# Where the tiles of a two-layer decoder trunk lie in SBUF

## The chip, the cores and the metric

The kernel runs on one core of one Trainium2 chip. What counts is its device time in microseconds. Several runs are timed, and the median is compared.

## What is computed

Two layers of a decoder trunk on one sequence of 512 tokens with 1,024 features, in float32. `c` is one vector of 1,024 that conditions the layer.

```python
for layer in range(DEPTH):
    mod = silu(c) @ w_ada[layer] + b_ada[layer]            # nine vectors of 1024
    sh1, sc1, g1, sh2, sc2, g2, sh3, sc3, g3 = split(mod)
    h = modulate(rmsnorm(x, norm_g[layer, 0]), sh1, sc1)
    x = x + 0.5 * g1 * ((silu(h @ w1) * (h @ w3)) @ w2)     # d_ff = 2816
    h = modulate(rmsnorm(x, norm_g[layer, 1]), sh2, sc2)
    proj = h @ w_in[layer]                                  # 3656 columns
    ...                                                     # 4 + 4 + 8 heads: block attention, top-k attention, stick-breaking
    x = x + g2 * (headnorm(concat(oa, ob, oc)) @ w_out[layer])
    h = modulate(rmsnorm(x, norm_g[layer, 2]), sh3, sc3)
    x = x + 0.5 * g3 * ((silu(h @ w1b) * (h @ w3b)) @ w2b)
```

## The kernel before

Everything is kept with features on the 128 partitions and the 512 tokens along them: the residual `xs` is 8 tiles of 128 x 512. To keep the precision of float32, each operand of a large product is split into two parts, a rounded one and the rest, both in the format fp32r: `whi` and `wlo` for weights, `hh` and `hl` for the normed input h, `gh` and `gl` for a chunk of d_ff. `mm3` (L309 to L311) then makes three matmuls of each block, whi with hh, whi with hl, wlo with hh. The weight part is loaded into PE, the other one moves through it, 512 columns at a time.

Weights come in pieces of 128 x 1,024. `fetch` (L269, L271) starts a DMA on SyncE's queue into one of three `raw` tiles, and ScalarE casts it to `whi`. `load_piece` (L281) lets VectorE subtract to get `wlo`. There are five buffers of each.

The order of time is: FFN 1 of layer 0, the mixing stage, FFN 2, the same for layer 1. A FFN has two halves of 11 chunks of d_ff. In a half each chunk is made by `mm3` from h (the first products, w1 and w3, 8 steps each), then by SiLU and a multiplication (L495, L497), and split into `gh` and `gl` (L500, L501). After 11 chunks the second product (w2) runs: for each of 8 output tiles of 128 features, `mm3` over the 11 chunks with `gh` and `gl` moving, and an update of `xs` (L513). The last two output tiles of the second half go in two column halves of 256. In between VectorE makes the modulation vectors from `adaw` tiles (L356). In the mixing stage an order written out by hand (PLAN) interleaves projections, score matmuls (L620, tiles `qk`), products with v (L664, tiles `att` moving and `v` loaded) and cumulative sums (L713, constants `rmat`).

SBUF is given out by pools. A pool is a stretch of the same byte range in all partitions. The pools that live all the time are stacked from low addresses up in the order in which they are opened; the pool of a stage (`fp` for the FFNs, `mp` for mixing) is opened above them, closed, and the next stage's pool takes the same bytes. A tile of the new pool waits until the old tiles under it are released. Within a pool each name gets its number of buffers times its size, in the order of first use. This gives, in bytes of a partition:

| tiles | before |
|---|---|
| xs, modulation vectors, constants (rmat, causal, ones) | 1,152 to 24,128 |
| raw, 3 x 4,096 | 24,128 to 36,416 |
| whi, 5 x 4,096 | 36,416 to 56,896 |
| wlo, 5 x 4,096 | 56,896 to 77,376 |
| hh, 8 x 2,048 | 77,376 to 93,760 |
| hl, 8 x 2,048 | 93,760 to 110,144 |
| small ones (nacc, rsqrt, sums) | 110,144 to 113,600 |
| FFN stage, from 113,600 | |
| gh, 14 x 2,048 | from 125,888 (first FFN), 138,176 (second and third), 134,080 (last) |
| gl, 14 x 2,048 | from 154,560, 166,848, 162,752 |
| adaw, 3 x 4,096 | 183,232 to 207,808; in the first stage six, from 117,696 |
| mixing stage, from 113,600 | |
| tok, v | 118,208 to 126,400; 126,528 to 142,912 |
| tf, qk, att | 142,912 to 157,248; 161,344 to 185,920; 185,920 to 214,592 |

The 14 slots of gh and gl (11 in use, 3 more) are handed out in turn: first slot 0, then from 13 downwards.

Of the kernel before, what the change touches and what calls it, by code (L numbers as in the profile page):

```python
# [19 lines left out]
F32R = mybir.dt.float32r  # L20
# [6 lines left out]
P = 128  # L27
S = 512
# [5 lines left out]
HALF = NF // 2  # L34
# [42 lines left out]
def col(i):  # L77
    return ((i * P, (i + 1) * P),)


def head_chunks(l, f):

    return list(range(4 if (l, f) == (0, 0) else 2))
# [99 lines left out]
class Net:  # L183
    def __init__(self, tc, ctx, io):
        self.tc, self.nc, self.ctx, self.io = tc, tc.nc, ctx, io
        self.n = 0
        self.cp = ctx.enter_context(tc.tile_pool(name="consts", bufs=1))
        self.wp = ctx.enter_context(tc.tile_pool(name="weights", bufs=1))
        self.hp = ctx.enter_context(tc.tile_pool(name="acts", bufs=1))
        self.sp = ctx.enter_context(tc.tile_pool(name="tiny", bufs=1))  # L190
        pp = ctx.enter_context(tc.tile_pool(name="psum", bufs=1, space=PSUM))
        self.bank = lambda tag, shape: self.t(pp, tag, shape, bufs=2)
        self.new_z = lambda: self.t(pp, "z", [P, 1024], bufs=3)
        self.xs = self.cp.tile([P, KC, S], F32, name="xs")
        self.x = [self.xs[:, k, :] for k in range(KC)]
        self.piece, self.fetched = -1, None
        self.queue, self.delayed = [], []
        self.logs = False
        self.order = ExitStack()
# [45 lines left out]
    def setup_late(self):  # L245
        nc, cp = self.nc, self.cp
        self.outg, self.qkg, self.gcol, self.rope = self.load("late", False)
        for p in (0, HD):
            nc.gpsimd.memset(self.gcol[p:p + RD], 1.0)
        for i in (0, 2):  # L250
            nc.gpsimd.tensor_scalar(self.gcol[:, :, i], self.gcol[:, :, i], HD ** -0.5, None, op0=ALU.mult)
        self.rmat = cp.tile([P, 4, P], F32R, name="rmat")
        m = self.t(self.wp, "raw", [P, 4, P], bufs=3)
        nc.sync.dma_start(m, self.io["cmat"][:, 0:4, :])
        nc.vector.tensor_copy(self.rmat, m)
        self.identr, self.tri, self.nones, self.maskc = (self.rmat[:, i, :] for i in range(4))
        self.ident = self.identr.bitcast(F32)
        self.causal = cp.tile([P, S], F32, name="causal")
        nc.gpsimd.memset(self.causal[:, :S - P], 0.0)
        nc.sync.dma_start(self.causal[:, S - P:], self.io["cmat"][:, 4, :])  # L260


    def fetch(self):

        nc = self.nc
        self.piece += 1
        n = sum(sum(b - a for a, b in blk[3]) for blk in PIECES[self.piece])
        raw = self.t(self.wp, "raw", [P, 1024], bufs=3)
        nc.sync.dma_start(raw[:, :n], self.io["w"][self.piece, :, :n])  # L269
        hi = self.t(self.wp, "whi", [P, 1024], F32R, bufs=5)  # L270
        nc.scalar.copy(hi[:, :n], raw[:, :n])  # L271
        self.fetched = n, raw, hi
# [206 lines left out]
    def ffn(self, l, f, filler, head):  # L479

        nc = self.nc
        full = slice(0, S)
        for hf in range(2):
            g = []
            for fc in range(hf * HALF, (hf + 1) * HALF):
                if fc in head_chunks(l, f):
                    pp = head[2 * fc:2 * fc + 2]
                else:
                    pp = self.z_banks(1)
                    for w, ps in zip(("ffn_w1", "ffn_w3"), pp):  # L490
                        for k in range(KC):
                            wt = self.weight(w, (l, f), k, col(fc))
                            self.mm3(ps, wt, self.h[k], k == 0, k == KC - 1)
                sl = self.t(self.fp, "sil", [P, S], bufs=2)
                nc.scalar.activation(sl, pp[0], AF.Silu)  # L495
                gf = self.t(self.fp, "gf", [P, S], bufs=2)
                nc.vector.tensor_mul(gf, sl, pp[1])  # L497
                hi = self.t(self.fp, "gh", [P, S], F32R, bufs=HALF + 3)
                lo = self.t(self.fp, "gl", [P, S], F32R, bufs=HALF + 3)
                nc.scalar.copy(hi, gf)  # L500
                nc.vector.tensor_sub(lo, gf, hi.bitcast(F32))  # L501
                g.append((hi, lo))
                if fc not in head_chunks(l, f):
                    next(filler, None)
            gate = self.mod[l, 2 if f == 0 else 8]

            def products(ps, ws, cs):
                for j in range(HALF):
                    self.mm3(ps[:, cs], ws[j], [p[:, cs] for p in g[j]],
                             j == 0 and cs.start == 0, j == HALF - 1, skip_group_check=cs != full)  # L510

            def update(m, ps, cs):
                nc.vector.scalar_tensor_tensor(self.x[m][:, cs], ps[:, cs], gate[:, m:m + 1],  # L513
                                               self.x[m][:, cs], op0=ALU.mult, op1=ALU.add)

            if hf == 1:
                self.norm_begin()
            w2 = lambda m: [self.weight("ffn_w2", (l, f), hf * HALF + j, col(m)) for j in range(HALF)]
            whole = KC - (TAIL if hf == 1 else 0)
            for m in range(whole):  # L520
                if m % 2 == 0:
                    pss = self.z_banks(1)
                ps = pss[m % 2]
                for j in range(HALF):
                    wt = self.weight("ffn_w2", (l, f), hf * HALF + j, col(m))
                    self.mm3(ps, wt, g[j], j == 0, j == HALF - 1)
                update(m, ps, full)
                if hf == 1:
                    yield m, full
            if whole == KC:  # L530
                continue
            last = list(zip(range(whole, KC), map(w2, range(whole, KC)), self.z_banks(TAIL)[::2]))
            for cs in HALVES:
                for m, ws, ps in last:
                    products(ps, ws, cs)
                    update(m, ps, cs)
                    yield m, cs

    def open_ffn(self, es):
        self.fp = es.enter_context(self.tc.tile_pool(name=self.name("fp"), bufs=1))  # L540
        self.temp = lambda: self.t(self.fp, "nt", [P, S], bufs=6)

# [616 lines left out]
```

## Time and profile before

| | |
|---|---|
| time, median of 3 runs | 2143.43 us (2143.17 to 2144.86) |
| the profiled execution, its own time | 2149.0 us |
| its span, first to last instruction | 2147.1 us |
| mean granted TensorE clock | 0.996 |
| PE busy | 2096.4 us, 98% |
| weight loads (PEld) | 1806.7 us, 84% |
| DVE busy | 1289.2 us, 60% |
| ACT busy | 837.4 us, 39% |
| DMA | 281.74 MB, mean 131 GB/s |

Times within a profile are microseconds from the start of the span. PE is the matmul side of TensorE, PEld its weight loads, which overlap PE. Matmuls are pipelined: the record of one is longer than the distance to the next, so the pace is read from start to start. A source line such as L309 is a line of a helper, which many callers share; the names of the tiles (out<-in) tell them apart.

### The profile page before, as it was taken

The page shows a single profiled execution, that of the slowest core. Times are in us where ns is not written, and L with a number is a line of the kernel's source. Part 1 is how long each engine was busy: PE and PEld are TensorE (multiplying, and loading weights), DVE is VectorE, ACT ScalarE, POOL GpSimd, SP SyncE. Part 2 cuts the span into 40 slices and gives each one's busy share as a digit, 9 for nine tenths or more (in the row PEclk, how much of TensorE's full clock was granted, in tenths as well). Part 3 has the DMA queues.
Part 4 walks back from the last instruction along what each step waited for, and adds up shares of the span by engine and source line. Part 5 has one row for each costly group of instructions (what it writes and reads, how often), then busy time and mean ns, then how long its engine had stood idle before and what let it go on. Part 6 is the DMA issues. An engine that isn't in the chain of part 4 may idle for free.

```text
span 2147.1 us, 28606 instructions
## 1 busy us (share of the span) xinstructions
PE 2096.4 (98%) x11280; PEld 1806.7 (84%) x11280; DVE 1289.2 (60%) x2425; ACT 837.4 (39%) x1347; POOL 3.5 (0%) x12
## 2 busy tenths in 40 slices
PE   6999999999999999999999999999999999999999
PEld 5888888888998888888898888888889998888888
DVE  8772753679978777275374333346899776333332
ACT  3321222467675432122242222324776644222220
POOL 0000000000000000000000000000000000000000
PEclk9999999999999999999999999999999999999999
DMA  7783853342333378386334333324334223333331
GB/s 297 264 283 98 265 171 89 103 107 67 100 91 103 112 262 279 98 269 199 90 105 132 98 98 96 93 82 122 91 84 106 74 71 108 98 89 99 98 102 56
DMA packets 86149, 281.74 MB, mean 131 GB/s; under 512 B 10752, under 2 KB 13312, under 8 KB 86016
## 3 DMA queue, kind: packets, MB, share of 16 engines
q1 hardware_dynamic: 84576, 277.83, 42.3%
q8 instruction: 88, 1.44, 0.3%
q10 hardware_dynamic: 1440, 2.10, 0.3%
q14 instruction: 45, 0.37, 0.1%
HBM read 256.55 MB, written 2.10 MB: 120 GB/s over the span
## 4 chain that ended last, share of the span: by engine, by line
PE 84%; DVE 10%; ACT 3%; DMA 2%; issue 1%; SPq 0%; ACTq 0%; DVEq 0%
PE z L309 23%; PE z L311 23%; PE z L310 23%; PE b L309 3%; PE b L311 3%; PE b L310 3%; DVE sc L862 2%; DVE m L861 2%; PE z L620 1%; DVE att L575 1%; DMA qk<-qk 1%; DVE wlo L281 1%; PE z L664 1%; PE z L713 1%; DVE tf L725 1%
## 5 line engine op out<-in xcount | busy, mean ns | idle before, releaser
L281 DVE TENSOR_TENSOR wlo<-raw,whi 128x1024 fp32r<-128x1024 f32 (+1 forms) x338 | 412.4, 1221 | 534.0 <-ACT whi L271 532.0
L271 ACT CAST whi<-raw 128x1024 fp32r<-128x1024 f32 (+1 forms) x338 | 354.3, 1049 | 863.1 <-PE z L310 791.8
L309 PE MATMUL z<-hh,whi 128*128 128x512 f32 (+1 forms) x1616 | 597.6, 371 | 6.9 <-DVE xs L996 3.9
L310 PE MATMUL z<-hl,whi 128*128 128x512 f32 (+1 forms) x1616 | 597.5, 370 | 0.5
L311 PE MATMUL z<-hh,wlo 128*128 128x512 f32 (+1 forms) x1616 | 596.4, 370 | 1.3 <-DVE wlo L281 1.3
L309 PEld LDWEIGHTS z<-hh,whi 128*128 128x128 f32 x1616 | 306.4, 190 | 59.1 <-DVE xs L996 4.3
L311 PEld LDWEIGHTS z<-hh,wlo 128*128 128x128 f32 x1616 | 306.3, 190 | 52.6 <-DVE wlo L281 1.8
L310 PEld LDWEIGHTS z<-hl,whi 128*128 128x128 f32 x1616 | 306.5, 190 | 52.0 <-DVE hl L437 1.3
L309 PE MATMUL z<-gh,whi 128*128 128x512 f32 (+1 forms) x792 | 293.7, 371 | 0.0
L310 PE MATMUL z<-gl,whi 128*128 128x512 f32 (+1 forms) x792 | 292.9, 370 | 0.0
L311 PE MATMUL z<-gh,wlo 128*128 128x512 f32 (+1 forms) x792 | 289.2, 370 | 0.0
L356 DVE CUSTOM_DVE_ANT_0 adaw<-adaw,silc 128x1024 f32<-128x1024 f32 x144 | 170.9, 1222 | 30.0 <-DMA adaw<-in_w_ada_dram 29.9
L309 PEld LDWEIGHTS z<-gh,whi 128*128 128x128 f32 x792 | 148.9, 188 | 29.7
L311 PEld LDWEIGHTS z<-gh,wlo 128*128 128x128 f32 x792 | 149.0, 188 | 27.7
L310 PEld LDWEIGHTS z<-gl,whi 128*128 128x128 f32 x792 | 149.0, 188 | 26.5
L309 PE MATMUL b<-whi,hh 128*128 128x256 f32 x544 | 156.7, 288 | 3.0 <-DVE v L654 2.1
L311 PE MATMUL b<-whi,hl 128*128 128x256 f32 x544 | 154.7, 284 | 0.0
L310 PE MATMUL b<-wlo,hh 128*128 128x256 f32 x544 | 154.6, 284 | 0.0
L513 DVE SCALAR_TENSOR_TENSOR xs<-z,mod,xs 128x512 f32<-128x512 f32 (+1 forms) x72 | 49.7, 691 | 124.7 <-PE z L311 124.6
L309 PEld LDWEIGHTS b<-whi,hh 128*128 128x128 f32 x544 | 104.8, 193 | 4.0 <-PE b L311 2.4
L310 PEld LDWEIGHTS b<-wlo,hh 128*128 128x128 f32 x544 | 104.8, 193 | 0.2
L311 PEld LDWEIGHTS b<-whi,hl 128*128 128x128 f32 x544 | 104.6, 192 | 0.0
(146 smaller groups left out, 2242.9 us busy)
## 6 DMA issues: line engine op xcount, KB each, us to landing
raw<-in_w_dram SPq DMA_DIRECT2D x332, 512.0 KB, 3.6
adaw<-in_w_ada_dram SPq DMA_DIRECT2D x144, 512.0 KB, 4.8
qk<-qk SPq DMA_DIRECT2D x144, 128.0 KB, 2.3
qk<-qk SPq DMA_DIRECT2D x24, 96.0 KB, 3.3
xs<-in_x_dram SPq DMA_DIRECT2D x4, 512.0 KB, 5.2
raw<-in_w_dram SPq DMA_DIRECT2D x4, 492.0 KB, 3.5
silc<-in_c_dram SPq DMA_DIRECT2D x3, 512.0 KB, 5.1
out_dram<-xs ACTq DMA_DIRECT2D x6, 256.0 KB, 2.0
```

Of the source, the lines that this page charges most:

```text
L271: nc.scalar.copy(hi[:, :n], raw[:, :n])
L281: self.nc.vector.tensor_sub(lo[:, :n], raw[:, :n], hi.bitcast(F32)[:, :n])
L309: mm(out, l[0], r[0], start=start, stop=False, **kw)
L310: mm(out, l[0], r[1], start=False, stop=False, **kw)
L311: mm(out, l[1], r[0], start=False, stop=stop, **kw)
L356: r = self.nc.vector.tensor_tensor_reduce(w, w, self.silc, 1.0, 0.0, op0=ALU.mult, op1=ALU.add, accum_out=m[:, j:j + 1])
L513: nc.vector.scalar_tensor_tensor(self.x[m][:, cs], ps[:, cs], gate[:, m:m + 1], self.x[m][:, cs], op0=ALU.mult, op1=ALU.add)
L575: nc.vector.tensor_sub(unit_sbuf(lo, u), src, unit_sbuf(hi.bitcast(F32), u))
L620: self.nc.tensor.matmul(out, a, b, start=start and i == 0, stop=stop and i == 1, skip_group_check=True)
L664: nc.tensor.matmul(outs[e][:, HT - w:], lhs, a[:, o:o + w], start=i + j == 0, stop=c == KEY_UNITS[u][-1][1] and j == 1, skip_group_check=True)
L861: nc.vector.max(m8, sc)
L862: nc.vector.match_replace(sc, m8, sc, TAKEN)
```

## The change

The pools are ordered anew. Three pools go to the far end, the high addresses, stacked downwards: `consts` (xs, modulation vectors, constants), a new pool `loads` for the raw weight pieces, and `tiny`. At the low end remain the weights' parts, then h, then for a FFN a new pool `gp` with gh and gl, and above it the other tiles of the stage. The mixing pool starts where `gp` does.

```diff
@@ -184,10 +184,13 @@
     def __init__(self, tc, ctx, io):
         self.tc, self.nc, self.ctx, self.io = tc, tc.nc, ctx, io
         self.n = 0
-        self.cp = ctx.enter_context(tc.tile_pool(name="consts", bufs=1))
+        far = lambda name: ctx.enter_context(tc.tile_pool(name=name, bufs=1, side="right"))
+        self.cp = far("consts")
+        self.rp = far("loads")
+        self.sp = far("tiny")
+
         self.wp = ctx.enter_context(tc.tile_pool(name="weights", bufs=1))
         self.hp = ctx.enter_context(tc.tile_pool(name="acts", bufs=1))
-        self.sp = ctx.enter_context(tc.tile_pool(name="tiny", bufs=1))
         pp = ctx.enter_context(tc.tile_pool(name="psum", bufs=1, space=PSUM))
         self.bank = lambda tag, shape: self.t(pp, tag, shape, bufs=2)
         self.new_z = lambda: self.t(pp, "z", [P, 1024], bufs=3)
@@ -250,7 +253,7 @@
         for i in (0, 2):
             nc.gpsimd.tensor_scalar(self.gcol[:, :, i], self.gcol[:, :, i], HD ** -0.5, None, op0=ALU.mult)
         self.rmat = cp.tile([P, 4, P], F32R, name="rmat")
-        m = self.t(self.wp, "raw", [P, 4, P], bufs=3)
+        m = self.t(self.rp, "raw", [P, 4, P], bufs=3)
         nc.sync.dma_start(m, self.io["cmat"][:, 0:4, :])
         nc.vector.tensor_copy(self.rmat, m)
         self.identr, self.tri, self.nones, self.maskc = (self.rmat[:, i, :] for i in range(4))
@@ -265,7 +268,7 @@
         nc = self.nc
         self.piece += 1
         n = sum(sum(b - a for a, b in blk[3]) for blk in PIECES[self.piece])
-        raw = self.t(self.wp, "raw", [P, 1024], bufs=3)
+        raw = self.t(self.rp, "raw", [P, 1024], bufs=3)
         nc.sync.dma_start(raw[:, :n], self.io["w"][self.piece, :, :n])
         hi = self.t(self.wp, "whi", [P, 1024], F32R, bufs=5)
         nc.scalar.copy(hi[:, :n], raw[:, :n])
@@ -495,8 +498,8 @@
                 nc.scalar.activation(sl, pp[0], AF.Silu)
                 gf = self.t(self.fp, "gf", [P, S], bufs=2)
                 nc.vector.tensor_mul(gf, sl, pp[1])
-                hi = self.t(self.fp, "gh", [P, S], F32R, bufs=HALF + 3)
-                lo = self.t(self.fp, "gl", [P, S], F32R, bufs=HALF + 3)
+                hi = self.t(self.gp, "gh", [P, S], F32R, bufs=HALF + 3)
+                lo = self.t(self.gp, "gl", [P, S], F32R, bufs=HALF + 3)
                 nc.scalar.copy(hi, gf)
                 nc.vector.tensor_sub(lo, gf, hi.bitcast(F32))
                 g.append((hi, lo))
@@ -537,6 +540,7 @@
                     yield m, cs
 
     def open_ffn(self, es):
+        self.gp = es.enter_context(self.tc.tile_pool(name=self.name("gp"), bufs=1))
         self.fp = es.enter_context(self.tc.tile_pool(name=self.name("fp"), bufs=1))
         self.temp = lambda: self.t(self.fp, "nt", [P, S], bufs=6)
```

In bytes of a partition this gives: whi 1,152 to 21,632, wlo to 42,112, hh to 58,496, hl to 74,880; gh 74,880 to 103,552, gl 103,552 to 132,224, the other tiles of the FFN from 132,224 (nt, the scratch of the norm, first from the second FFN on). In the mixing stage all tiles lie 38,720 lower than before: v 87,808 to 104,192, tf 104,192 to 118,528, qk 122,624 to 147,200, att 147,200 to 175,872. The far end begins near 190,600. No instruction, size or number of buffers is changed.

## Rows read from the trace of the kernel before

**Rows 1.** The page: PE's busy time, share, instructions; the chain by engine.
```profile
PE 2096.4 (98%) x11280; PEld 1806.7 (84%) x11280; DVE 1289.2 (60%) x2425; ACT 837.4 (39%) x1347; POOL 3.5 (0%) x12
...
PE 84%; DVE 10%; ACT 3%; DMA 2%; issue 1%; SPq 0%; ACTq 0%; DVEq 0%
```

**Rows 2.** The view of waits, PE alone: total, times, longest.
```profile
PE b L415 <- DVE nacc L407: 11.4, 1, 11.4
```

**Rows 3.** Line L309, h moving: count, min/median/max ns, first and last start.
```profile
L309 PE MATMUL z<-hh,whi x119: 389/389/390, 1119.7 to 1200.0; 128*128 128x512 f32 x119
...
L309 PEld LDWEIGHTS z<-hh,whi x118: 187/188/188, 1120.2 to 1199.7; 128*128 128x128 f32 x118
...
L309 PE MATMUL z<-hh,whi x163: 388/389/390, 1269.7 to 1379.8; 128*128 128x512 f32 x163
```

**Rows 4.** Line L309, gh moving, in two FFNs; columns as in 3.
```profile
L309 PE MATMUL z<-gh,whi x71: 387/393/405, 1206.8 to 1255.7; 128*128 128x512 f32 x71
...
L309 PE MATMUL z<-gh,whi x70: 387/393/404, 146.7 to 194.9; 128*128 128x512 f32 x70
```

**Rows 5.** Windows, us: PE, PEld, DVE, ACT, POOL busy; clock, DMA share, GB/s.
```profile
905.00:1015.00 110.00, 110.00 (x487) 91.11 (x486) 70.42 (x102) 32.37 (x41) 0.00 (x0) 1.00 0.71 234
...
1270.00:1380.00 110.00, 110.00 (x487) 91.14 (x486) 37.41 (x40) 32.20 (x40) 0.00 (x0) 1.00 0.34 100
...
1206.00:1256.00 50.00, 50.00 (x217) 40.31 (x216) 16.46 (x17) 10.29 (x11) 0.00 (x0) 1.00 0.33 95
```

**Rows 6.** Timeline of PE where gh follows h: start, length us.
```profile
1204.72 0.40 PE L309 MATMUL z<-gh,whi 128*128 128x512 f32 x1
...
1206.11 0.40 PE L309 MATMUL z<-gh,whi 128*128 128x512 f32 x1
```

**Rows 7.** Groups of lines by form, PE.
```profile
L309 PE MATMUL z<-gh,whi 128*128 128x512 f32 x616 | 243.6, 395 | 0.0
...
L309 PE MATMUL z<-gh,whi 128*128 128x256 f32 x176 | 50.0, 284 | 0.0
...
L309 PE MATMUL z<-hh,whi 128*128 128x512 f32 x1296 | 505.0, 390 | 2.8 <-ACT hh L436 2.8
```

**Rows 8.** Timeline of PE in 256-wide stretches, gh and gl, then h.
```profile
1434.83 0.28 PE L310 MATMUL z<-gl,whi 128*128 128x256 f32 x1
...
1435.90 0.28 PE L310 MATMUL z<-gl,whi 128*128 128x256 f32 x1
...
712.00 0.28 PE L309 MATMUL z<-hh,whi 128*128 128x256 f32 x1
...
714.16 0.28 PE L309 MATMUL z<-hh,whi 128*128 128x256 f32 x1
```

**Rows 9.** Timeline of PE around h matmuls among and behind gh ones.
```profile
1258.51 0.40 PE L309 MATMUL z<-hh,whi 128*128 128x512 f32 x1
...
1259.67 0.39 PE L309 MATMUL z<-gh,whi 128*128 128x512 f32 x1
...
1267.37 0.39 PE L311 MATMUL z<-hh,wlo 128*128 128x512 f32 x1
...
1268.53 0.39 PE L310 MATMUL z<-hl,whi 128*128 128x512 f32 x1
```

**Rows 10.** Timeline of PE in the mixing stage, h between qk.
```profile
1523.21 0.39 PE L309 MATMUL b<-hh,whi 128*128 128x512 f32 x1
...
1524.38 1.08 PE L620 MATMUL z<-qk,qk 128*128 128x512 f32 x4
```

**Rows 11.** Lines L356 and L664, the latter's weight loads; columns as in 3.
```profile
L356 DVE CUSTOM_DVE_ANT_0 adaw<-adaw,silc x144: 1217/1222/1232, 11.3 to 1138.4; 128x1024 f32<-128x1024 f32 x144
...
L664 PEld LDWEIGHTS z<-att,v x192: 186/192/193, 452.1 to 682.8; 128*128 128x128 f32 x192
```

**Rows 12.** Lines L620 and L406 around the first border of stages.
```profile
L620 PE MATMUL z<-qk,qk x52: 220/338/483, 601.7 to 672.4; 128*128 128x512 f32 x14, 128*128 128x384 f32 x14, 128*128 128x256 f32 x12, 128*128 128x128 f32 x12
...
L406 ACT ACTIVATE nt<-xs x14: 400/418/419, 696.5 to 720.3; 128x256 f32<-128x256 f32 x14
```

## The prediction

> **What bounds the kernel now.** I read the page first. PE is busy 98% of the span, and 84% of the chain that ended last lies on it [rows 1]. So the end is set by the sum of PE's matmul periods, and a change of addresses matters if it changes how long a matmul takes or makes PE wait. PE's own waits are small: the largest is 11.4 us, at the start [rows 2].
>
> Next I looked at PE's pace inside the FFN, from start to start, because a record's length (0.39 us) overlaps its neighbours. In the first products, where h moves against w1 and w3, line L309 comes 119 times from 1119.7 to 1200.0 us, and each time stands for three matmuls: 80.3 / 118 / 3 = 226.8 ns. The stretch at 1270 us gives 110.1 / 162 / 3 = 226.5 ns [rows 3]. In the second product, where gh and gl move against w2, it is (1255.7 - 1206.8) / 70 / 3 = 232.9 ns, and in the first FFN (194.9 - 146.7) / 69 / 3 = 232.9 ns [rows 4]. Engine, width (512 columns), weight buffers and granted clock (1.00 [rows 5]) are the same; the moving tiles differ.
>
> Traffic does not explain it. Over 110 us, 487 matmuls start at a DMA share of 0.71 with DVE busy 70 us, and 487 at a share of 0.34 with DVE busy 37 us; the second product is slower at a share of 0.33 [rows 5]. The step comes with the tile: the first gh matmul follows an h one at 1204.72 us, and six steps from there to 1206.11 us are 232 ns each [rows 6].
>
> What differs is the place. By the layout in front, h lies at bytes 77,376 to 110,144 of a partition and the chunks lie at 125,888 and up in every FFN. Neither group drifts within itself. I take it as a step somewhere above 110,144: near tiles cost 226.7 ns, far ones 232.8, 6.1 ns more.
>
> **The change, part by part.** No instruction is added or removed; only addresses, and the releases that hang on them, move.
>
> *gh and gl.* All of both are far before. Now they lie at 74,880 to 103,552 and 103,552 to 132,224. They move in 616 x 3 = 1,848 matmuls of 512 columns and 176 x 3 = 528 of 256 [rows 7]. If all become near, the wide ones give 1,848 x 6.1 ns = 11.3 us. The narrow ones go the other way: nine gl and gh steps from 1434.83 to 1435.90 us are 118.9 ns each, while eighteen h steps from 712.00 to 714.16 us are 120.0 ns [rows 8], so 528 x 1.1 ns = 0.6 us is lost. Sum: 10.7 us less.
>
> *How much of gl is near.* The bounds of the step are 110,144 (h, fast) and, if each matmul pays for its own tile alone, 125,888 (the first gh, slow). But a near matmul close behind a far one is slow too. Behind a second product the next h matmuls start at 1267.37 to 1268.53 us, five steps of 232 ns, before the old pace is back, and five h matmuls that stand among gh ones, from 1258.51 to 1259.67 us, take 232 ns each throughout [rows 9]. So one gl in three may have kept the whole second product slow, and then the gh of the first FFN says nothing of its own address: the step may lie as high as 154,560, where gl began there, and the new 132,224 may be wholly near. If only the last one or two of gl's fourteen slots are far, each of them keeps its triple and the five matmuls behind it slow, and I get 8.5 to 9 us instead of 10.7. I take 9.5, between the two. If the step lies low, at 114,000, five slots are near. Of the 33 matmuls of one output tile (11 chunks by 3) at most 5 x 3 - 3 = 12 are then fast, and fewer where the 11 chunks in use leave some of the five out. Counted over the order in which slots are handed out it is 23% of 11.3 us: 2.6. At 121,000 it is 4.7, at 125,000 about 6.5.
>
> [...]
>
> *Weights' parts and h* move from 36,416 to 110,144 down to 1,152 to 74,880: near before and after, 0. The two buffers of a weight's parts lie 20 KB apart and h spans 32 KB, and the stretches of [rows 3] run at one pace through all of them, so a still lower place should give nothing; the bound is that drift, 0.3 ns of 226.8, or 1 us over h's matmuls.
>
> *What goes to the far end.* xs, raw and the modulation columns are touched by ACT, DVE and DMA. DVE's product with adaw takes 1217 to 1232 ns in 144 tiles that lie anywhere from 117,696 to 207,808 [rows 11]; that is flat, so 0 for DVE, and the bound is the 1%. No row shows ACT or a DMA on one size at both ends. I take 0 for them too, because ACT is busy 32 of 110 us and DMA 0.34 to 0.71 of the time in these stages [rows 5]: some per cent on either stay covered. The constants that PE reads (identity, triangle, ones) become far. Loads of the far v as weights take 192 ns, of h's weights from near tiles 188 [rows 3, 11]; over a few hundred matmuls of the mixing stage 4 ns is at most 2 us. I take 0, because these loads partly run under the matmul before.
>
> *Mixing tiles.* They shift down by 38,720. v comes near, but v is only a weight. qk (122,624 up) stays at the step or above it, att (147,200 up) above it unless the step is very high. Taken as 0; if they turn near, a few hundred matmuls gain up to 6 ns, 1 to 2 us.
>
> *Releases at stage borders.* The new pools lie over other old tiles. The one nearest to the path is nt, the scratch of the next norm: at 132,224 up it lies over qk, whose last read starts at 672.4 us, while nt is first written at 696.5 us [rows 12]. So 24 us cover it, and 0. Without that cover, each microsecond that nt comes late would hold ACT's squares and PE behind them as long, in both layers. Every load behind SP's queue keeps its order, and raw keeps its three slots.
>
> **Sum.** The profiled execution's own time is 2149.0 us (span 2147.1); 2149.0 - 9.5 = 2139.5 for such an execution. The median of the timed runs is 5.6 us lower, so 2143.4 - 9.5 = 2134 there. ACT and DVE have room in the second product (10 and 16 of 50 us [rows 5]), so PE's gain reaches the end whole.
>
> **The rivals.**
> *The step lies low* (0.20): 2 to 7 us, 2136.5 to 2141.5. For it: the longer period outlasts the far tile. About half of this chance is a gain under 0.2%.
> *Each matmul pays alone* (0.08): with the step below 125,888, gh is near and 5 to 10 of gl's slots too: 8.1 to 9.5 us, 2134 to 2135.5. Against it: the five h matmuls among gh ones.
> *No effect of the place* (0.17): the second product is slow for what it is: 2143.4, within 1 us. [...] For it: h among gh is slow too. Against it: five h matmuls between qk ones, in another stage, 1523.21 to 1524.38 us, take 234 ns each [rows 10], and qk is far (161,344 up).
> *Start alignment instead of place* (0.04), on the other side: all h tiles start 1,600 past a multiple of 2,048, all g tiles 960 past one; after the change both start at 1,152. If 1,152 is a slow one, h pays too: 1,296 x 3 = 3,888 matmuls [rows 7] by 6.1 ns is 23.7 us, 2167. It decides if h's period leaves 226.7. Against it: qk starts at 1,600 as h does and is found with the 234 ns. If 1,152 is a fast one, the time is that of the likeliest case.
> *Crossing the step costs* (0.04): five slow steps behind a crossing are 26 ns. If each far gl between two near gh paid 26 + 6 for its triple instead of 18, the 616 triples, 0.7 of them far, would lose 6 us, less 2.6 won: 2147. It needs the step below some 115,000; the h run of five, which costs no more than a far run, speaks against it.
>
> **How the numbers follow.** The likeliest case, all or nearly all of both tiles near, has 0.47: 2134, its own range 2132 to 2135.5. A measurement of this kernel tells about 0.2%, 4.3 us, from no change. Faster by more than that: 0.47 + 0.08 + half of 0.20 = 0.65. Within: the other half and 0.17, 0.27. Slower: 0.04 + 0.04 = 0.08, the crossing case counted whole. The range runs from 2131.5 (all near, and 2 us from qk and att) to 2143.5: it takes in the low step and half of no effect, and leaves out 0.08 on the slow side, the other half of 0.17 and a little below.
>
> **What would show it.** L309 with gh at 226.7 ns from start to start instead of 232.9 in all four FFNs, and 120 instead of 119 in its 256-wide tail; L309 with h unchanged. A step within gl shows as stretches of 227 and of 233 ns within one output tile, in the slots' order. Alignment shows in h. PE's waits stay as they are. I am wrong if gh stays at 232.9, or if PE gets a new wait where a stage begins, at some 400, 690, 1460 or 1750 us.

## The result and the profile after

The change makes the kernel faster: the median is 2134.13 us (4 runs, 2130.51 to 2135.47) against 2144.14 us before on the same chip (4 runs, 2143.17 to 2145.40). The ratio is 0.995, with a 95% interval of 0.9933 to 0.9968. The prediction said 2134.0. Line numbers of the changed kernel are three higher: `mm3` is L312 to L314.

The page of the kernel after, as in [rows 1]:

```profile
PE 2080.5 (98%) x11280; PEld 1799.6 (84%) x11280; DVE 1288.9 (60%) x2425; ACT 836.2 (39%) x1347; POOL 3.7 (0%) x12
...
PE 84%; DVE 10%; ACT 3%; DMA 2%; issue 1%; SPq 0%; ACTq 0%; DVEq 0%
```

PE is the bound as it was. Its waits are about what they were: the longest is the one of [rows 2], and the other two shown came to 7.0 and 4.1 us before. Total in us, times, longest:

```profile
PE b L418 <- DVE nacc L410: 11.4, 1, 11.4
PE b L426 <- DVE ry L343: 7.2, 6, 2.2
PE z L668 <- DVE att L579: 4.2, 6, 1.1
```

What has changed is the pace. Line L312 over one stretch of the second FFN, first the products with h and then the second product; columns as in [rows 3]:

```profile
L312 PE MATMUL z<-hh,whi x174: 388/389/390, 893.7 to 1011.3; 128*128 128x512 f32 x174
L312 PE MATMUL z<-gh,whi x55: 388/389/396, 1012.0 to 1048.8; 128*128 128x512 f32 x55
```

The products with h take (1011.3 - 893.7) / 173 / 3 = 226.6 ns from start to start, as in [rows 3]. The second product now takes (1048.8 - 1012.0) / 54 / 3 = 227.2 ns, where [rows 4] gave 232.9. First and last start are given to 0.1 us, so the latter figure, and each pace of 55 rows below, is good to 0.6 ns. At the change from h to gh, where six steps took 1.39 us in [rows 6], they now take 1.36 us, 227 ns each (timeline of PE; start, length):

```profile
1195.37 0.39 PE L312 MATMUL z<-gh,whi 128*128 128x512 f32 x1
...
1196.73 0.39 PE L312 MATMUL z<-gh,whi 128*128 128x512 f32 x1
```

In terms of the prediction's sum that is 1,848 x (232.9 - 227.2) ns = 10.5 us. The matmuls of 256 columns take back 0.6 us of it, as is shown further below; that leaves 9.9, and the timed medians differ by 10.0. The two spans differ by more, 2147.1 - 2131.0 = 16.1 us. The rest, 6.2 us, goes with the granted clock in the mixing stages and at their borders. Windows of the kernel before (columns as in [rows 5]); the first two lines are a pause, the last two what follows it:

```profile
392.00:394.00 2.00, 1.61 (x11) 1.34 (x9) 1.95 (x21) 0.35 (x3) 0.00 (x0) 1.00 0.51 98
394.00:396.00 2.00, 0.16 (x2) 0.19 (x3) 1.77 (x5) 0.43 (x3) 0.00 (x0) 1.00 0.41 164
396.00:398.00 2.00, 2.00 (x14) 1.99 (x14) 1.72 (x5) 1.58 (x6) 0.00 (x0) 0.76 0.58 160
398.00:400.00 2.00, 2.00 (x10) 2.00 (x9) 2.00 (x6) 0.94 (x4) 0.00 (x0) 0.50 0.29 111
```

PE was idle for 2.23 us, up to 395.84 us, and then the clock stood at 0.50. In that execution there are five such places, at 396, 458, 718, 1460 and 1780 us, each behind a pause of PE of 1.84 to 2.23 us and with a clock of 0.50 to 0.53 in its lowest window of 2 us. In the profiled execution of the kernel after there is one with PE at work. Its windows around the same work as above, and around the one place:

```profile
380.00:400.00 20.00, 17.60 (x123) 16.95 (x123) 18.64 (x64) 12.62 (x29) 0.00 (x0) 1.00 0.24 76
...
1440.00:1460.00 20.00, 17.77 (x117) 17.35 (x116) 17.16 (x54) 11.16 (x28) 0.00 (x0) 0.91 0.28 81
```

Summed over windows of 20 us in which PE works, (1 - clock) x 20 is 8.4 us before and 1.8 us after. The difference of 6.6 us is about what the spans differ by beyond the 9.9. The pause alone doesn't decide: in the same work after, PE is idle for 2.23 us too, with a clock of 1.00 behind it (timeline of PE, the pause in brackets, before and after):

```profile
395.84 0.40 PE L423 MATMUL b<-rmat,ry 128*128 128x128 f32 x2 [2.23 <-DVE ry L340]
...
393.29 0.40 PE L426 MATMUL b<-rmat,ry 128*128 128x128 f32 x2 [2.23 <-DVE ry L343]
```

It goes by execution and not by kernel: of 13 executions of the kernel before on another chip, the one with a mean clock of 1.000 took 2140.58 us and the one with 0.996 took 2148.89 us. The medians are therefore the numbers to compare, and the pace inside a FFN, where the clock is 1.00 in both kernels (every window of 20 us from 740 to 1440 us), shows the cause.

### The profile page after: what moved, and what is told of

It is laid out like the page before. It is cut to its first block, busy times and chain, and to the rows that moved or that the text cites. A ratio compares the mean times of both kernels' runs of the same rounds, so it can differ in the third digit from the quotient of the medians.

```text
span 2131.0 us, 28603 instructions
## 1 busy us (share of the span) xinstructions
PE 2080.5 (98%) x11280; PEld 1799.6 (84%) x11280; DVE 1288.9 (60%) x2425; ACT 836.2 (39%) x1347; POOL 3.7 (0%) x12
## 3 DMA queue, kind: packets, MB, share of 16 engines
q10 hardware_dynamic: 1440, 2.10, 0.3%
## 4 chain that ended last, share of the span: by engine, by line
PE 84%; DVE 10%; ACT 3%; DMA 2%; issue 1%; SPq 0%; ACTq 0%; DVEq 0%
PE z L312 23%; PE z L314 23%; PE z L313 23%; PE b L312 3%; PE b L314 3%; PE b L313 3%; DVE sc L866 2%; DVE m L865 1%; PE z L624 1%; DVE wlo L284 1%; DVE att L579 1%; PE z L668 1%; DMA qk<-qk 1%; PE z L717 1%; DVE tf L729 1%
## 5 line engine op out<-in xcount | busy, mean ns | idle before, releaser
L312 PE MATMUL z<-hh,whi 128*128 128x512 f32 (+1 forms) x1616 | 596.0, 370 | 6.9 <-DVE xs L1000 3.9
L314 PE MATMUL z<-hh,wlo 128*128 128x512 f32 (+1 forms) x1616 | 595.1, 369 | 2.6 <-DVE wlo L284 2.6
L312 PEld LDWEIGHTS z<-hh,whi 128*128 128x128 f32 x1616 | 304.9, 189 | 58.9 <-DVE xs L1000 4.3
L314 PEld LDWEIGHTS z<-hh,wlo 128*128 128x128 f32 x1616 | 304.6, 189 | 54.0 <-DVE wlo L284 3.5
L312 PE MATMUL z<-gh,whi 128*128 128x512 f32 (+1 forms) x792 | 291.0, 367 | 0.0
L314 PE MATMUL z<-gh,wlo 128*128 128x512 f32 (+1 forms) x792 | 286.3, 366 | 0.0
L312 PEld LDWEIGHTS z<-gh,whi 128*128 128x128 f32 x792 | 149.4, 189 | 27.4 <-DVE xs L516 0.7
L314 PEld LDWEIGHTS z<-gh,wlo 128*128 128x128 f32 x792 | 149.4, 189 | 24.5
L312 PE MATMUL b<-whi,hh 128*128 128x256 f32 x544 | 156.5, 288 | 3.0 <-DVE v L658 2.1
L314 PE MATMUL b<-whi,hl 128*128 128x256 f32 x544 | 154.6, 284 | 0.0
L312 PEld LDWEIGHTS b<-whi,hh 128*128 128x128 f32 x544 | 104.5, 192 | 4.1 <-PE b L314 2.4
L314 PEld LDWEIGHTS b<-whi,hl 128*128 128x128 f32 x544 | 104.5, 192 | 0.0
```

Of the source, the lines that this page charges most:

```text
L312: mm(out, l[0], r[0], start=start, stop=False, **kw)
L314: mm(out, l[1], r[0], start=False, stop=stop, **kw)
```

## The experiments

The prediction took the cause to be the place of a tile: near is fast, far is slow. All kernels below compute the whole result; a `pad` is an unused tile that only shifts what lies above it. "Pace" is worked out as above, over the same stretch of the second FFN if nothing else is said. The first four ran on one chip, with a median before of 2143.33 us (13 runs, 2140.58 to 2148.89).

**The other pools alone.** From the kernel after, with gh and gl put back into the stage's pool:

```diff
-                hi = self.t(self.gp, "gh", [P, S], F32R, bufs=HALF + 3)
-                lo = self.t(self.gp, "gl", [P, S], F32R, bufs=HALF + 3)
+                hi = self.t(self.fp, "gh", [P, S], F32R, bufs=HALF + 3)
+                lo = self.t(self.fp, "gl", [P, S], F32R, bufs=HALF + 3)
...
-        self.gp = es.enter_context(self.tc.tile_pool(name=self.name("gp"), bufs=1))
```

> The pools are ordered as after the change, but gh and gl stay in the FFN's stage pool: gh from 87,168 and gl from 115,840 to 144,512 in the first FFN, gh from 99,456 and gl from 128,128 to 156,800 in the second and third, 4,096 bytes less in the last. Place, with a step between 132,224 and 154,560: h and gh near, the upper slots of gl far in the second to fourth FFN; the period in the second product lies between 226.7 and 232.9 ns and is the longer one only where slots above the step are in use, so the step can be read from the slots; the time lies between 2134 and 2141 us. Start alignment: all these tiles start at 1,152 past a multiple of 2,048 as after the change, so 226.7 ns everywhere and 2134 us.

Measured: 2132.73 us (2131.29 to 2134.97), ratio 0.9946 [0.9930, 0.9963]. Its line L312 in the same stretch:

```profile
L312 PE MATMUL z<-gh,whi x55: 389/389/395, 1011.5 to 1048.3; 128*128 128x512 f32 x55
```

That is 227.2 ns. Over the FFNs gh here begins at 87,168 to 99,456 and gl ends as high as 156,800, and every second product runs at 226.7 to 227.8 ns. Tiles that lie well above 125,888, where [rows 4] showed 232.9, are fast. No step of place is left below 156,800.

**The pool for gh and gl alone.** The reverse: the kernel before, with a pool `gp` opened ahead of `fp` and gh and gl in it.

```diff
+        self.gp = es.enter_context(self.tc.tile_pool(name=self.name("gp"), bufs=1))
         self.fp = es.enter_context(self.tc.tile_pool(name=self.name("fp"), bufs=1))
```

> The kernel before with the new pool for gh and gl alone: gh from 113,600 to 142,272, gl from 142,272 to 170,944 in every FFN; h and weights where they were. Place with a slow tail behind each far tile: gl is far or nearly so, and one far matmul in three keeps the whole second product at 232 to 233 ns; 2142 to 2144 us. Place with each matmul paying for its own tile: two of three become near where gh lies below the step, about 228.8 ns on average and 2137 us. No effect of the place: 2144 us as well, with h and gh unlike for another reason.

Measured: 2144.91 us (10 runs, 2141.82 to 2146.38), ratio 1.0001 [0.9992, 1.0011].

```profile
L309 PE MATMUL z<-gh,whi x55: 390/393/404, 1018.4 to 1056.0; 128*128 128x512 f32 x55
```

232.1 ns here, and 232.6 to 232.9 over the longer runs of the timeline. gh now begins at 113,600 and still is slow. By itself this agrees with a low step, and also with no effect of the place; together with the run before, in which tiles of this range are fast up to 156,800, a low step is out.

**The start of the tiles alone.** The kernel before, with 192 unused bytes at the bottom of the FFN's pool, so that gh and gl stay at 126,080 and above but start 1,152 past a multiple of 2,048, as they do after the change:

```diff
         self.fp = es.enter_context(self.tc.tile_pool(name=self.name("fp"), bufs=1))
+        self.t(self.fp, "pad", [P, 48])
```

> The kernel before with 192 unused bytes at the bottom of the FFN's pool, so that gh and gl start at 1,152 past a multiple of 2,048, as they do after the change, but stay at 126,080 and above. Place: nothing changes, 232.9 ns in the second product, 2144 us. Start alignment: 226.7 ns there and about 2133.5 us.

Measured: 2136.22 us (2132.84 to 2137.99), ratio 0.9957 [0.9942, 0.9972].

```profile
L309 PE MATMUL z<-gh,whi x55: 388/392/398, 1014.1 to 1051.2; 128*128 128x512 f32 x55
```

229.0 ns (229.1 to 229.5 over the longer runs): neither 227 nor 233. Both theories miss it. Tiles with the same start in memory, 128,128 for one, are at 227 two runs further up and at 229 here. The moving tile's own address, by place or by alignment, can't be the cause. What differs between the two kernels in those products is the other operand: the weights' parts start at 64 past a multiple of 512 here (36,416), at 128 there (1,152).

**h at the far end.** The kernel after, with `self.hp = far("acts")`: h at 157,856 to 190,624, gh and gl from 42,112 to 99,456.

> The kernel after the change with h's pool at the far end: hh and hl from 157,856 to 190,624; weights' parts stay at 1,152 to 42,112, gh and gl come down to 42,112 to 99,456, qk and att to 89,856 to 143,104. Place of the moving tile: the first products go from 226.7 to 232.9 ns, 3,888 to 4,512 wide matmuls by 6.1 ns, 24 to 27 us more than the kernel after the change, about 2159 us; the second product stays at 226.7 ns. Something that belongs to the second product and not to the place: the first products stay at 226.7 ns, 2134 us.

Measured: 2156.99 us (2156.00 to 2159.47), ratio 1.0058 [1.0043, 1.0073].

```profile
L312 PE MATMUL z<-hh,whi x174: 393/394/397, 903.4 to 1024.5; 128*128 128x512 f32 x174
L312 PE MATMUL z<-gh,whi x55: 389/389/397, 1025.2 to 1062.0; 128*128 128x512 f32 x55
```

h goes to 233.3 ns, gh is at 227.2. The sum holds: 3,888 x (233.3 - 226.7) ns = 25.7 us lost, less 10.5 won by gh and gl, is 15.2 us more than before; measured 13.7. Alone this could be read as place. But h has also moved against the weights: its start lies 32 past the weights' start, counted modulo 256.

So a third theory was formed. What counts is the distance from the start of the weights' part to the start of the moving tile, modulo some power of two. Before, weights and h both start at 64 past a multiple of 512, and gh and gl at 448, since the small tiles (3,456 bytes) lie below them. After, all start at 128. The next four ran on one chip, with a median before of 2144.25 us (7 runs, 2142.32 to 2145.31).

**128 bytes.** The kernel before with a pad of 128 bytes instead of 192; gh and gl stay at 126,016 and above, but now start at 64 past a multiple of 512, as its weights do:

```diff
         self.fp = es.enter_context(self.tc.tile_pool(name=self.name("fp"), bufs=1))
+        self.t(self.fp, "pad", [P, 32])
```

> The kernel before with 128 unused bytes at the bottom of the FFN's pool: gh and gl stay at 126,016 and above, but start at the same place within 512 bytes (64) as the weights' parts do. Relation, the theory formed from the first four runs (the period depends on how the moving tile and the weights' parts lie to each other within 512 bytes, 226.7 ns where they agree): 226.7 ns in the second product of all four FFNs and 2133 to 2135 us, the whole gain. Place, or the address of the moving tile alone (with 192 bytes more, 229 ns): 229 to 233 ns and 2136 us or more.

Measured: 2134.08 us (2133.03 to 2135.29), ratio 0.9951 [0.9935, 0.9968].

```profile
L309 PE MATMUL z<-hh,whi x174: 389/389/389, 894.0 to 1011.7; 128*128 128x512 f32 x174
L309 PE MATMUL z<-gh,whi x55: 389/389/397, 1012.3 to 1049.1; 128*128 128x512 f32 x55
```

227.2 ns. One unused tile of 128 bytes gives the whole gain of the new order.

**Three sweeps.** The kernel after, with a pad under h and one under gh in each stage, to set the distance; each ran once. The edit of the first:

```diff
+        self.pads = [0, 0, 64, 192]
...
+        self.t(self.hp, "pad", [P, 16])
...
         self.gp = es.enter_context(self.tc.tile_pool(name=self.name("gp"), bufs=1))
+        pad = self.pads.pop(0)
+        if pad:
+            self.t(self.gp, "pad", [P, pad // 4])
```

The second has pads of 0, 416, 64, 256 and 128 bytes under h; the third 0, 256, 352, 192 and 256 bytes under h. The second entry counts for the first FFN, the third for the two in the middle, the fourth for the last.

> The kernel after the change with unused bytes before h and before gh, so that, against the weights' parts and within 512 bytes, h starts 64 further; gh and gl 64 further in the first FFN, 128 in the second and third, 256 in the last. Relation: h leaves 226.7 ns for about 229, as gh did with 64; the second products go to 229 in the first FFN and to two other periods between 227 and 234 in the others. If 128 or 256 gives 226.7 again, the period of the pattern is that and not 512. Place: 226.7 ns everywhere.

> As the run before, with h 128 further, gh and gl 32 in the first FFN, 192 in the second and third, 384 in the last. Relation: h shows the period that gh shows with 128 there; gh about 233.4 with 32 (as h had it with 32 at the far end) and 232.8 with 384 (as in the kernel before). Place: 226.7 ns everywhere.

> As the run before, with h 256 further, gh and gl 0 in the first FFN, 96 in the second and third, 448 in the last. Relation: 226.7 ns in the first FFN's second product, other periods where it is 96 and 448, h as gh with 256. Place: 226.7 ns everywhere.

Measured: 2145.19, 2168.45 and 2143.31 us. The pace is read from line L314, which is the first of `mm3` in these kernels. First sweep: h, then gh in the first FFN, the second and the last:

```profile
L314 PE MATMUL z<-hh,whi x174: 394/394/394, 204.2 to 323.0; 128*128 128x512 f32 x174
L314 PE MATMUL z<-gh,whi x55: 388/392/398, 323.7 to 360.8; 128*128 128x512 f32 x55
...
L314 PE MATMUL z<-gh,whi x55: 388/393/404, 1017.0 to 1054.7; 128*128 128x512 f32 x55
...
L314 PE MATMUL z<-gh,whi x55: 389/389/395, 2079.2 to 2115.9; 128*128 128x512 f32 x55
```

Second sweep: h in the first FFN and in the third, then gh in the first, the third and the last:

```profile
L314 PE MATMUL z<-hh,whi x174: 390/393/404, 207.6 to 328.2; 128*128 128x512 f32 x174
L314 PE MATMUL z<-hh,whi x174: 392/395/398, 1279.1 to 1400.2; 128*128 128x512 f32 x174
...
L314 PE MATMUL z<-gh,whi x55: 393/396/400, 328.9 to 366.7; 128*128 128x512 f32 x55
...
L314 PE MATMUL z<-gh,whi x55: 388/393/398, 1400.9 to 1438.7; 128*128 128x512 f32 x55
...
L314 PE MATMUL z<-gh,whi x55: 387/392/404, 2101.5 to 2139.2; 128*128 128x512 f32 x55
```

Third sweep: h in the first FFN, then gh in the first, the third and the last:

```profile
L314 PE MATMUL z<-hh,whi x174: 388/390/390, 203.4 to 321.1; 128*128 128x512 f32 x174
L314 PE MATMUL z<-gh,whi x55: 388/389/396, 321.8 to 358.5; 128*128 128x512 f32 x55
...
L314 PE MATMUL z<-gh,whi x55: 391/393/400, 1381.3 to 1419.1; 128*128 128x512 f32 x55
...
L314 PE MATMUL z<-gh,whi x55: 393/394/395, 2076.4 to 2114.2; 128*128 128x512 f32 x55
```

Set in order of the distance, modulo 512, with the kernels above (paces of gh from these rows, plus or minus 0.6 ns; of h, plus or minus 0.2):

| moving start minus weights' start | pace, ns | where |
|---|---|---|
| 0 | 226.7; 227 | h before and after; gh after, 128-byte pad, third sweep |
| 32 | 233.3; 233.3 | h at the far end; gh, second sweep |
| 64 | 228.9; 229 | h, first sweep; gh, first sweep and 192-byte pad |
| 96 | 233.3 | gh, third sweep |
| 128 | 232.4 or 233.3; 232.7 | h, second sweep; gh, first sweep |
| 192 | 233.3 | gh, second sweep |
| 256 | 226.8; 226.5 | h, third sweep; gh, first sweep |
| 384 | 232.7; 232.9 | gh, second sweep; gh before |
| 448 | 233.3 | gh, third sweep |

At 128, h takes 232.4 ns in four of its eight stretches and 233.3 in the other four, which the distance doesn't explain. Otherwise h and gh agree wherever both were tried, in four FFNs and at places from 42,112 (gh with h at the far end) to 195,648 (gl in the middle FFNs of the 128-byte run). Place, which says 226.7 ns everywhere, fails in all three sweeps; the relation had said 229 at 64, 233.4 at 32 and 232.8 at 384 ahead of them, and 229, 233.3 and 232.7 were measured. The times follow: in the third sweep three of the four second products are slow, 1,386 matmuls by 6.1 ns or 8.5 us, and it took 9.2 us more than the kernel after. At the distances tried the result repeats with 256: 0 and 256 are fast (226.5 to 227 ns), 128 and 384 alike slow (232.4 to 233.3 ns), 192 and 448 too (233.3 ns each). And it goes by the distance and not by an address: gh at 64 past a multiple of 512 is fast, 227.2 ns, where the weights are at 64 (128-byte pad) and slow, 233.3 ns, where they are at 128 (third sweep, last FFN); gh at 128 takes 227.2 ns with weights at 128 and 229.0 ns with weights at 64.

## Why the prediction came out as it did

**The time was met, its cause was not: that the number fits is luck.** The wide matmuls of the second products went from 232.9 to 227.2 ns, 10.5 us, where the prediction had 11.3 if all of them gained. It took 9.5 in place of 10.7, to allow for a few slow slots of gl; there were none, and 10.5 less the 0.6 of the narrow matmuls is what the medians show. But the sum only needs gh and gl to take on the pace of h, whatever the reason. "Start alignment" with 1,152 as a fast start gives the same time, so the time can't tell the two apart. PE's gain reached the end whole, as the bound by PE said. h stayed at its pace, and so did PE's waits. The release that was named as nearest to the path kept its cover: the last read of qk starts at 666.0 us and the first write of nt there at 690.0, 24 us as in [rows 12].

**The step that failed is "What differs is the place".** It was taken because two groups of tiles at two paces also lay at two ends. The prediction saw that their starts differ too, 1,600 and 960 past a multiple of 2,048, and put that aside since qk "starts at 1,600 as h does and is found with the 234 ns". Those 234 ns are steps of h matmuls that stand between qk ones [rows 10], not a pace of qk, and they speak neither for place nor against alignment. They are there after the change as well, with other addresses: five steps from 1510.22 to 1511.39 us, 234 ns each. The other-pools run has gl up to 156,800 at 227 ns, and the 128-byte run has the old places, shifted by 128 bytes, at the new pace. The bounds of the step between 110,144 and 154,560, and with them the rivals of a low step, of each matmul paying for its own tile and of a cost at a crossing, answered a question that didn't arise. The near end gave the gain because three pools left it, which put weights, h, gh and gl at one alignment.

**"No effect of the place" (0.17) was right in what it says of place and wrong in its time**, because another property of the address paid. The trace shows no idle time before the gh matmuls (0.0 us in [rows 7]), but matmuls of one shape took 226.7 to 233.3 ns by the distance of their two operands in memory.

**"Start alignment" (0.04) was the nearest and still not it.** It looked at the moving tile alone, modulo 2,048. The 192-byte run gives exactly the start that it called fast or slow and gets something between, 229.0 ns. Nor could its sign, that alignment shows in h, have told: h kept its distance of 0 from the weights, and its pace of 226.6 ns. Its warning was sound, though: the run with h at the far end, at a distance of 32, shows 3,888 matmuls paying 6.6 ns each, 13.7 us more than before in all, although gh and gl had gained 10.5 there.

**The narrow matmuls lost what the prediction said.** In the tail of each of the first three FFNs, 74 steps of 256 columns take 8.77 us before, 118.5 ns each, and 8.87 to 8.88 us after, 120.0 ns. In the third FFN, first and last before, then after (timeline of PE):

```profile
1433.30 0.28 PE L309 MATMUL z<-gh,whi 128*128 128x256 f32 x1
1442.07 0.28 PE L311 MATMUL z<-gh,wlo 128*128 128x256 f32 x1
...
1421.21 0.28 PE L312 MATMUL z<-gh,whi 128*128 128x256 f32 x1
1430.09 0.28 PE L314 MATMUL z<-gh,wlo 128*128 128x256 f32 x1
```

In the tail of the last FFN, 41 rows of 256 columns span 14.4 us after, (2127.4 - 2113.0) / 40 / 3 = 120 ns, and before, from 2129.0 to 2143.4 us, 120 ns as well:

```profile
L312 PE MATMUL z<-gh,whi x41: 282/283/284, 2113.0 to 2127.4; 128*128 128x256 f32 x41
```

So 396 of the 528 narrow matmuls lose 1.5 ns, which is the 0.6 us of the sum. At a distance of 64 the tail takes 117.8 ns in the first FFN of the first sweep (74 steps, 370.28 to 379.00 us) and 118 in the last FFN of the 192-byte run (41 rows, 2117.9 to 2132.1 us). At 256 columns, then, neither is slower than the 120 ns at distance 0, and two tails at one distance differ: at 384, before, those of the first three FFNs take 118.5 ns and that of the last 120.

**What stays open.** Why the distance counts isn't shown. Each matmul has its weight load (187 to 188 ns in [rows 3]), and the loads run beside the matmuls (91.14 us of loads in 110.00 us of matmuls without a gap, [rows 5]); that the two operands get in each other's way is the author's estimate from this, and no run takes the loads away. The record of the load itself grows no longer: with h at the far end, at 233.3 ns, it takes 187 to 188 ns too.

```profile
L312 PEld LDWEIGHTS z<-hh,whi x156: 187/187/188, 895.0 to 1011.0; 128*128 128x128 f32 x156
```

The narrow matmuls, which take 120 ns at distance 0 and 117.8 at 64, don't fit that estimate as it stands. No run moves the weights' parts alone, either: between the kernels with weights at 64 and those with weights at 128, other pools moved as well, though the matmuls of a second product read none of these, only the weights' parts, gh and gl. Nor is it shown why five matmuls behind a slow stretch keep its 232 ns [rows 9], or why h between qk matmuls takes 234 ns [rows 10], though by the table h stands well to its own weights.

## What to carry to other kernels

Where a stream of equal matmuls of 512 columns runs at two paces (226.7 and 232.9 ns here), compare the addresses of both operands, modulo small powers of two, before reading a near and a far end into them: a pad of 128 bytes did here what a new order of the pools did (2134.08 and 2134.13 us). A tiny pool of 3,456 bytes between the weights and the moving tiles set their distance here, so the order of pools changed the time, by 10.0 us, through remainders that no one chose. One run that holds the place and changes the alignment, and one that does the reverse, tell the two apart; a time that fits doesn't, when two causes give the same time. Distance 0 was among the best here for 512 columns (226.7 ns); at 256 columns it was not (120 ns, and 117.8 at 64).

## What was not expected of the hardware

- In these runs the pace of 512-column matmuls, each with its own weight load, went with the distance of the two operands' starts in a partition: 226.5 to 227 ns at 0 or 256 bytes, 229 at 64, 232.4 to 233.3 at 128, 232.7 to 232.9 at 384, 233.3 at 32, 96, 192 and 448. At 256 columns 0 was slower than 64: 120 ns and 117.8.
- Place itself showed no effect between 42,112 and 195,648: at distance 0, gh and gl took 227.2 ns at both ends.
- The granted clock fell to 0.50 to 0.53 (windows of 2 us) behind some pauses of PE and not behind others of the same length (2.23 us in both profiled kernels): five times in one execution and once in the other. That is worth 6.6 us between the spans, two thirds of the effect under study.
